# Transformer block on one Trainium2 core: odd channel tiles of the MLP input used as operands where they lie, squares on ScalarE, the first half's residual later, the last stores behind loads

## The chip, the cores and the metric

The kernel runs on one core of a Trainium2 chip. Its time is the device time of one execution, in microseconds (us). The engines are TensorE (PE in the profile, with its weight loads as PEld), VectorE (DVE), ScalarE (ACT), GpSimd (POOL) and SyncE (SP). DMAs are issued from three queues here: SP's (q1 in the profile), ACT's (q10) and POOL's (q0). All move their bytes on the core's 16 DMA engines.

## The reference, cut to what matters

One decoder layer in float32 over 512 positions with 2048 channels. The attention and recurrence in its first part are the same in both kernels. The change is in the MLP and in the residual behind it:

```python
h = rms_norm(x1, norm2_w) * (1 + scale) + shift      # adaLN: scale, shift, gate from c
f = jnp.square(jax.nn.relu(h @ w_ff1))               # 2048 -> 8192
x = x1 + gate * (f @ w_ff2)                          # 8192 -> 2048
```

## The kernel before, in words

Every float32 product is made of three float32r matmuls: an operand is split into `hi` (a cast on ACT) and `lo` (the rest, by a subtraction on DVE), and PE sums hi x hi, hi x lo and lo x hi. A matmul is 128x128 against 128x512.

From about 1000 us on the kernel runs the MLP. FF1 gives 16 groups `g` of 512 hidden columns.

- *Plain groups*, g = 0 to 3, about 1016 to 1190 us (`first_hidden`, then `hidden(g)`). `h2[k]` is the hi/lo pair of channel tile k of the normalised input (128 channels x 512 positions), `uT[k]` the same in float32. A group multiplies the 16 tiles with weights `wraw`, cast to `whi` (ACT) and `wlo` (DVE), into four PSUM banks. Relu goes to an SBUF tile, DVE squares it into `fs`.
- *Forms.* The other 12 groups of FF1 and all of FF2 are done by a Strassen-Winograd scheme with seven products of half-size blocks. Its left operands are seven forms of the four blocks a11, a12, a21, a22 of an activation tile. `make_forms` computes them in `fs`, splits them two at a time into `part` tiles (`plain_stage`, 7 buffers) and stores the parts in DRAM from POOL's queue: `f_hid`, `f_lod` for the hidden groups, `h_hid`, `h_lod` for the input. `input_forms(u)`, u = 0 to 3, does it for four channel tiles of the input each. These tasks are generators; `tick()` takes the next step of one after each channel tile of groups 1 to 3.
- *Form products.* `product(i, ...)` runs product i, in the order 1, 5, 6, 7, 3, 4, 2 (the very first block: 1, 3, 5, 6, 7, 4, 2). It is four turns u of 12 matmuls. `operand` loads the forms from DRAM on POOL's queue as `Fh` and `Fl`, half of them at a time, into four `fp` buffers. For FF1, the forms of products 4 and 2 are loaded once, as `Rh` and `Rl` of 1 MB each (pool `res`), and kept. `part` casts a weight block `raw` (loaded by SP, 512 KB) to `vhi` on ACT and takes `vlo` on DVE. The blocks are b11, b12, b21, b22; b11 and b12 are replaced by sums on DVE in the course of a round, product 2 takes b21 and product 3 takes b22. FF1 has six such blocks of two groups (to about 1680 us). FF2 has two halves `q` of the output columns with four rounds `c` each, a round being seven products.
- *Turn.* After an FF1 block, `turn` transposes the two new groups, squares them (on ACT already) and calls `make_forms` in place: the lo parts are stored from `fs2` itself. The last turn, for group 14, runs in the first round of FF2.
- *Residual.* `residual_in(q)` loads from ACT's queue the gate (one DMA of 128x1024) and eight tiles `d` of x1 (128x512 each), which `finish` in the last round of the half needs. It is issued after the last copy of round c = 0 (`done`).

PE's order is the order of the code. The other engines' order is set by a scheduler that estimates times. A `dma_start` stands in the instruction queue of the engine that issues it: while it waits, all behind it on that engine wait. A DMA also waits for the DMA before it with the same completion semaphore: POOL's DMAs use eight semaphores in turn (DMASW0 to 7), and SP's and ACT's share another eight (DMAHW0 to 7).

Of the kernel before, what the change touches and what calls it, by code (L numbers as in the profile page):

```python
# [15 lines left out]
P = 128  # L16
# [28 lines left out]
def hybrid_block(ctx, tc, x, c, positions, norm1_w, w_ada, b_ada, w_in, q_norm_w, k_norm_w,  # L45
# [92 lines left out]
    def to_cols(accs, dst):  # L138
# [6 lines left out]
        pc = bank("pc")  # L145
# [77 lines left out]
    ph = ctx.enter_context(ExitStack())  # L223
    hp = ph.enter_context(tc.tile_pool(name="hp", bufs=1, side="right"))
# [7 lines left out]
    def pair(i):  # L232

        return [hp.tile([P, S], F32R, name=f"{c}{i}", tag=f"{c}{i}") for c in ("hi", "lo")]
# [5 lines left out]
    for i in range(NK):  # L240
        pair(i)
# [25 lines left out]
    spare.extend(hp.tile([P, 512], F32, name="araw", tag=f"{c}{k}") for k in range(8, NK) for c in ("hi", "lo"))  # L267
# [678 lines left out]
    def first_hidden():  # L946
# [28 lines left out]
        run_all(to_cols(accs, bias))  # L975
# [12 lines left out]
    def hidden(g):  # L988
# [7 lines left out]
        for j in range(4):  # L996
            r = xr.tile([P, 512], F32, name="relu", tag="x")
            act.activation(r, banks[j], AF.Relu)
            yield r
# [10 lines left out]
    def forms_in_dram(name, n):  # L1010
        return [dr.tile([n * FORMS * P, 512], F32, name=f"{name}_{c}d").rearrange("(g i p) n -> g i p n", i=FORMS, p=P)
                for c in ("hi", "lo")]

    fparts, hparts = forms_in_dram("f", NG), forms_in_dram("h", KG)

    def make_forms(fs, dst, g, stage, in_place=False):
# [7 lines left out]
        for a, b in ((0, 2), (2, 4), (4, 6), (6, 7)):  # L1024
            hi = stage()[:, 0:b - a]
            lo = fs[:, a:b].bitcast(F32R) if in_place else stage()[:, 0:b - a]
            act.copy(hi, fs[:, a:b])
            dve.tensor_tensor(lo, fs[:, a:b], hi.bitcast(F32), op=ALU.subtract)
            for d, t in zip(dst, (hi, lo)):
                pool.dma_start(d[g, a:b].rearrange("i p n -> p i n"), t.rearrange("p i a t -> p i (a t)").bitcast(F32))  # L1030
            yield
# [7 lines left out]

    def plain_forms():  # L1040
        return stg.tile([P, FORMS, 2, 256], F32, name="fs", bufs=1)

    def plain_stage():
        return stg.tile([P, 2, 2, 256], F32R, name="part", bufs=7)

    def input_forms(u):
        fs = plain_forms()
        for j in range(4):
            act.copy(block(fs, j), halves(uT[4 * u + j]))
        yield  # L1050
        yield from make_forms(fs, hparts, u, plain_stage)
# [3 lines left out]
    for g in range(PLAIN):  # L1055
# [5 lines left out]
        for j, r in enumerate(rs):  # L1061
            dve.tensor_tensor(block(fs, j), halves(r), halves(r), op=ALU.mult)
# [9 lines left out]
    ph.close()  # L1072
# [10 lines left out]
    res_ = ctx.enter_context(ExitStack())  # L1083
    res = res_.enter_context(tc.tile_pool(name="res", bufs=1, side="right", reuse_waits="tile"))


    slot_of = {1: 1, 2: 3, 3: 6, 4: 2, 5: 4, 6: 5, 7: 0}
    order = (1, 5, 6, 7, 3, 4, 2)
    first_order = (1, 3, 5, 6, 7, 4, 2)
    NC = NG // KG  # L1090
    kept = {}

    def operand(src, c, i):

        def load(t, d, g):
            n = t.shape[1]
            pool.dma_start(t.rearrange("p g a t -> p g (a t)").bitcast(F32),  # L1097
                           d[g:g + n, slot_of[i]].rearrange("g p n -> p g n"))
            return t
# [280 lines left out]
```

## Time and profile before

| | |
|---|---|
| median of 3 runs (lowest, highest) | 2307.28 us (2306.57, 2311.78) |
| profiled execution, its span | 2306.17 us, 2304.4 us |
| mean granted TensorE clock | 0.994 |
| DMA bytes | 606.71 MB, mean 263 GB/s |
| POOL's queue q0 | 262.60 MB |
| SP's queue q1 | 332.54 MB |
| ACT's queue q10 | 9.44 MB |

The span is that of the recorded instructions; 1.8 us of the execution lie around it. A row of the list of waits names the waiting engine, operation and line, then what it waited for: total us, times, longest. In a timeline row stand start, duration, engine, line, operation, out<-in, and in brackets the idle time before it and what ended it. "ACTq" and "SPq" are DMA issues in those queues. A row of DMA issues ends with size and time from issue to landing.

### The profile page before, as it was taken

What the parts mean: (1) busy time and instruction counts of PE and PEld (TensorE: products, weight loads), DVE (VectorE), ACT (ScalarE), POOL (GpSimd) and SP (SyncE); (2) the same over time, 40 slices, a digit from 0 to 9 for tenths busy, and PEclk for the clock granted to TensorE, in tenths of its full rate; (3) what the DMA queues carried; (4) which work ended last, traced back from release to release, by engine and by line L of the source; (5) the groups of instructions that cost most, each with busy time, mean ns of one, the idle gap of its engine ahead of it and who ended that gap; (6) DMA issues with size and microseconds to landing.
All of it is one profiled execution on the core that took longest, in us unless ns stands there. A gap on an engine that the chain in (4) does not pass through costs nothing.

```text
span 2304.4 us, 33163 instructions
## 1 busy us (share of the span) xinstructions
PE 2230.5 (97%) x11769; PEld 1829.2 (79%) x11769; DVE 1825.9 (79%) x2773; ACT 1103.0 (48%) x1958; POOL 458.1 (20%) x668
## 2 busy tenths in 40 slices
PE   4999999999999999999999999999998999999999
PEld 3787877888778888888887888888887888888887
DVE  6899777677776565669767988988895789967878
ACT  5555434433344553457644555565563333344332
POOL 1000022000230000001332323323232222222221
PEclk9999999999999999999999999999999999999999
DMA  9798455556545256746999799889889987999784
GB/s 327 249 337 314 123 176 156 176 162 215 178 149 182 74 186 218 259 132 220 366 382 382 252 341 355 301 297 380 310 295 369 339 288 262 364 336 335 277 302 165
DMA packets 264695, 606.71 MB, mean 263 GB/s; under 512 B 23284, under 2 KB 44032, under 8 KB 264528
## 3 DMA queue, kind: packets, MB, share of 16 engines
q1 hardware_dynamic: 186800, 332.54, 42.8%
q0 software_dynamic: 72832, 262.60, 31.1%
q10 hardware_dynamic: 4896, 9.44, 1.2%
q8 instruction: 93, 1.52, 0.3%
q14 instruction: 74, 0.61, 0.1%
HBM read 522.68 MB, written 81.81 MB: 262 GB/s over the span
## 4 chain that ended last, share of the span: by engine, by line
PE 56%; DMA 16%; DVE 14%; issue 10%; POOL 2%; ACT 1%; SPq 0%; DVEq 0%; POOLq 0%; ACTq 0%
PE f L1160 9%; PE f L1161 9%; PE f L1159 9%; DMA araw<-in_w_ada_dram 7%; PE prj L198 4%; PE prj L200 4%; PE prj L199 4%; DMA f_lod<-fs 3%; DVE acc L129 3%; PE f L208 2%; PE f L206 2%; PE f L207 2%; DVE vlo L1146 2%; DVE wlo L40 2%; PE prj L206 2%
## 5 line engine op out<-in xcount | busy, mean ns | idle before, releaser
L1145 ACT CAST vhi<-raw 128x1024 fp32r<-128x1024 f32 x392 | 412.8, 1055 | 547.1 <-PE f L1161 434.3
L1146 DVE TENSOR_TENSOR vlo<-raw,vhi 128x1024 fp32r<-128x1024 f32 x392 | 477.4, 1225 | 154.3 <-ACT vhi L1145 153.5
L1159 PE MATMUL f<-vhi,Fh 128*128 128x512 f32 x1376 | 537.6, 391 | 8.3 <-DMA Fh<-h_hid 3.6
L1160 PE MATMUL f<-vlo,Fh 128*128 128x512 f32 x1376 | 538.1, 391 | 3.0 <-DVE vlo L1146 3.0
L1161 PE MATMUL f<-vhi,Fl 128*128 128x512 f32 x1376 | 537.2, 390 | 2.1 <-DMA Fl<-f_lod 1.3
L39 ACT CAST whi<-wraw 128x512 fp32r<-128x512 f32 (+1 forms) x368 | 219.8, 601 | 449.3 <-PE prj L200 323.7
L198 PE MATMUL prj<-whi,hi 128*128 128x512 f32 x896 | 365.0, 407 | 1.3 <-ACT gg L698 1.3
L200 PE MATMUL prj<-whi,lo 128*128 128x512 f32 x896 | 351.5, 392 | 0.0
L199 PE MATMUL prj<-wlo,hi 128*128 128x512 f32 x896 | 350.8, 391 | 0.0
L40 DVE TENSOR_TENSOR wlo<-wraw,whi 128x512 fp32r<-128x512 f32 (+1 forms) x368 | 245.1, 670 | 111.7 <-ACT whi L39 107.1
L129 DVE SCALAR_TENSOR_TENSOR acc<-araw,sc,acc 128x512 f32<-128x512 f32 (+1 forms) x392 | 253.9, 678 | 98.5 <-DMA araw<-in_w_ada_dram 97.2
L1159 PEld LDWEIGHTS f<-vhi,Fh 128*128 128x128 f32 x1376 | 259.0, 188 | 63.3 <-issue 7.1
L1160 PEld LDWEIGHTS f<-vlo,Fh 128*128 128x128 f32 x1376 | 259.0, 188 | 61.7 <-DVE vlo L1146 8.3
L1161 PEld LDWEIGHTS f<-vhi,Fl 128*128 128x128 f32 x1376 | 259.1, 188 | 56.7 <-DMA Fl<-f_lod 1.8
L1129 DVE TENSOR_TENSOR raw<-raw,raw 128x1024 f32<-128x1024 f32 x224 | 269.5, 1223 | 1.8 <-DMA raw<-in_w_ff_dram 1.5
L198 PEld LDWEIGHTS prj<-whi,hi 128*128 128x128 f32 x896 | 169.4, 189 | 36.5 <-ACT gg L698 1.6
L200 PEld LDWEIGHTS prj<-whi,lo 128*128 128x128 f32 x896 | 168.9, 188 | 36.8
L199 PEld LDWEIGHTS prj<-wlo,hi 128*128 128x128 f32 x896 | 169.6, 189 | 32.4 <-DVE wlo L40 0.4
L1097 POOL DMA_DIRECT2D Fh<-f_hid x112 | 80.9, 722 | 428.3 <-PE f L1161 414.8
L208 PE MATMUL f<-hi,wlo 128*128 128x512 f32 x256 | 99.8, 390 | 0.6 <-DVE wlo L40 0.6
L206 PE MATMUL f<-hi,whi 128*128 128x512 f32 x256 | 100.2, 391 | 0.0
L207 PE MATMUL f<-lo,whi 128*128 128x512 f32 x256 | 99.6, 389 | 0.0
(306 smaller groups left out, 2956.9 us busy)
## 6 DMA issues: line engine op xcount, KB each, us to landing
raw<-in_w_ff_dram SPq DMA_DIRECT2D x224, 512.0 KB, 10.0
araw<-in_w_ada_dram SPq DMA_DIRECT2D x384, 256.0 KB, 4.3
Fh<-f_hid POOLq DMA_DIRECT2D x112, 512.0 KB, 6.5
Fl<-f_lod POOLq DMA_DIRECT2D x112, 512.0 KB, 7.4
wraw<-in_w_in_dram SPq DMA_DIRECT2D x104, 512.0 KB, 4.1
Fh<-h_hid POOLq DMA_DIRECT2D x60, 512.0 KB, 6.8
Fl<-h_lod POOLq DMA_DIRECT2D x60, 512.0 KB, 8.3
f_hid<-part POOLq DMA_DIRECT2D x48, 512.0 KB, 8.1
```

What stands on the lines that cost most here:

```text
L39: nc.scalar.copy(hi, src)
L40: (eng or nc.vector).tensor_tensor(lo, src, hi.bitcast(F32), op=ALU.subtract)
L129: dve.scalar_tensor_tensor(acc, raw[:, k - k0], vec[:, k:k + 1], acc, op0=ALU.mult, op1=ALU.add)
L198: pe.matmul(banks[ti], lhsT=hi[:, ts], rhs=whi, start=first, stop=False)
L199: pe.matmul(banks[ti], lhsT=hi[:, ts], rhs=wlo, start=False, stop=False)
L200: pe.matmul(banks[ti], lhsT=lo[:, ts], rhs=whi, start=False, stop=last)
L1129: dve.tensor_tensor(dst, a, b, op=ALU.subtract)
L1145: act.copy(hi, src)
L1146: split_done.append(dve.tensor_tensor(lo, src, hi.bitcast(F32), op=ALU.subtract))
L1159: pe.matmul(banks[t], lhsT=fh[u][:, a, ts], rhs=whi[:, a], start=first, stop=False)
L1160: pe.matmul(banks[t], lhsT=fh[u][:, a, ts], rhs=wlo[:, a], start=False, stop=False)
L1161: pe.matmul(banks[t], lhsT=fl[u][:, a, ts], rhs=whi[:, a], start=False, stop=end)
```

## The change

It has four parts.

1. *Odd tiles in place.* In the input's form layout, the odd channel tiles hold a22 and a12, which are the operands of products 4 and 2 as they are. `operand` now hands out slices of `h2`'s odd tiles for these, so the `Rh`/`Rl` loads and the pool `res` go. The pool `hp` of the pairs is split: `hp0` (even tiles) is freed after the plain groups, `hp1` (odd tiles) is kept until the end of the FF1 products. a11 is stored straight from the even tiles; only four forms per u are computed (in `xf`) and split. `part` has 5 buffers instead of 7.
2. *Squares on ACT.* The plain groups' Relu goes from PSUM straight to `fs`, and ACT squares there (`squared`, now shared with `turn`); DVE multiplies group 0's banks by `rbc` in place.
3. *Last stores behind loads.* In FF2 a task step is taken once a product instead of four times, and the stores of group 14 are ordered behind the latest operand load (`behind=loads`).
4. *Residual.* `residual_in(q)` stands at the end of round c = 1 for q = 0 (before: c = 0) and c = 0 for q = 1, and it is ordered behind the last `vhi` cast of product 2 (`cast_done[-1]`) instead of behind the last copy of that product's result.

```diff
-    hp = ph.enter_context(tc.tile_pool(name="hp", bufs=1, side="right"))
+    hp1 = ph1.enter_context(tc.tile_pool(name="hp1", bufs=1, side="right"))
+    hp0 = ph0.enter_context(tc.tile_pool(name="hp0", bufs=1, side="right"))
...
         for j in range(4):
-            r = xr.tile([P, 512], F32, name="relu", tag="x")
-            dve.tensor_tensor(r, banks[j], rbc, op=ALU.mult)
-            act.activation(r, r, AF.Relu, bias=bias[:, j:j + 1])
-            yield r
+            dve.tensor_tensor(banks[j], banks[j], rbc, op=ALU.mult)
+            yield banks[j], bias[:, j:j + 1]
...
+    def split_out(fs, a, b, stage, in_place, dst, behind=None):
+        hi = stage()[:, 0:b - a]
+        lo = fs[:, a:b].bitcast(F32R) if in_place else stage()[:, 0:b - a]
+        act.copy(hi, fs[:, a:b])
+        dve.tensor_tensor(lo, fs[:, a:b], hi.bitcast(F32), op=ALU.subtract)
+        with tc.issue_after(behind[-1].ins) if behind else ExitStack():
+            for d, t in zip(dst, (hi, lo)):
+                pool.dma_start(d.rearrange("i p n -> p i n"), t.rearrange("p i a t -> p i (a t)").bitcast(F32))
...
+    def squared(fs, banks):
+        for j in (0, 2, 1, 3):
+            act.activation(block(fs, j), halves(banks[j][0]), AF.Relu, bias=banks[j][1])
+            if j in (2, 3):
+                v = fs[:, (j - 2) * 2:(j - 2) * 2 + 2]
+                act.activation(v, v, AF.Square)
...
-        return stg.tile([P, 2, 2, 256], F32R, name="part", bufs=7)
+        return stg.tile([P, 2, 2, 256], F32R, name="part", bufs=5)
     def input_forms(u):
-        fs = plain_forms()
-        for j in range(4):
-            act.copy(block(fs, j), halves(uT[4 * u + j]))
-        yield
-        yield from make_forms(fs, hparts, u, plain_stage)
+        xf = stg.tile([P, 4, 2, 256], F32, name="xf", bufs=1)
+        s1, s2, s4, s3 = (xf[:, i] for i in range(4))
+        for a in range(2):
+            ev, od = (halves(uT[4 * u + 2 * a + e]) for e in range(2))
+            a21, a11, a22, a12 = ev[:, 0], ev[:, 1], od[:, 0], od[:, 1]
...
+            for d, t in zip(hparts, h2[4 * u + 2 * a]):
+                pool.dma_start(d[u, 1, :, a * 256:(a + 1) * 256], t[:, 256:512].bitcast(F32))
+        yield
+        for a in (0, 2):
+            split_out(xf, a, a + 2, plain_stage, False, [d[u, 4 + a:6 + a] for d in hparts])
+            yield
...
         if src is hparts and i in (4, 2):
-            if i not in kept:
-                kept[i] = [load(res.tile([P, KG, 2, 256], F32R, name=f"R{n}{i}"), d, 0) for d, n in zip(src, "hl")]
-            return [[t[:, u] for u in range(KG)] for t in kept[i]]
+            half = slice(256, 512) if i == 2 else slice(0, 256)
+            return [[[h2[4 * u + 2 * a + 1][j][:, half] for a in range(2)] for u in range(KG)] for j in range(2)]
...
-                tick()
+                if u == KG - 1 or src is hparts:
+                    tick()
...
-        yield from make_forms(fs, fparts, 2 * b + n, stage, True)
+        yield from make_forms(fs, fparts, 2 * b + n, stage, True, loads if 2 * b + n == NG - 2 else None)
...
                     if c == 0:
-                        done = act.copy(accs7[i, t], banks[t])
+                        act.copy(accs7[i, t], banks[t])
...
-            if c == 0:
-                with tc.issue_after(done.ins):
+            if c == 1 - q:
+                with tc.issue_after(cast_done[-1].ins):
                     residual_in(q)
```

Three places show what moves. First POOL's queue where the form products of FF1 begin, before. Numbers behind a name tell tiles apart; the two pairs at the top belong to the second product, the R tiles to products 4 and 2, the last pair to the third product. `part_12106` and so on hold the forms of group 3.

```order
L1097 DMA Fh_12302<-h_hid_10578 128x2x512
L1097 DMA Fl_12304<-h_lod_10579 128x2x512
L1097 DMA Rh4_12618<-h_hid_10578 128x4x512
L1097 DMA Rl4_12620<-h_lod_10579 128x4x512
L1097 DMA Rh2_12721<-h_hid_10578 128x4x512
L1097 DMA Rl2_12723<-h_lod_10579 128x4x512
L1030 DMA f_hid_10576<-part_12106 128x2x512
L1030 DMA f_hid_10576<-part_12112 128x2x512
L1030 DMA f_lod_10577<-part_12107 128x2x512
L1030 DMA f_hid_10576<-part_12118 128x2x512
L1030 DMA f_lod_10577<-part_12113 128x2x512
L1097 DMA Fh_12372<-h_hid_10578 128x2x512
```

The same place after the change (`Fh_12316` is the third product's first half, `Fh_12320` its second):

```order
L1125 DMA Fh_12246<-h_hid_10581 128x2x512
L1125 DMA Fl_12248<-h_lod_10582 128x2x512
L1023 DMA f_hid_10579<-part_12053 128x2x512
L1125 DMA Fh_12316<-h_hid_10581 128x2x512
L1125 DMA Fl_12318<-h_lod_10582 128x2x512
L1023 DMA f_hid_10579<-part_12059 128x2x512
L1023 DMA f_lod_10580<-part_12054 128x2x512
L1023 DMA f_hid_10579<-part_12065 128x2x512
L1023 DMA f_lod_10580<-part_12060 128x2x512
L1125 DMA Fh_12320<-h_hid_10581 128x2x512
L1125 DMA Fl_12322<-h_lod_10582 128x2x512
```

The R loads are gone, and the third product's first pair stands ahead of all stores of group 3 but one, where it stood behind seven of them.

Next POOL's queue in the first round of FF2 (q = 0, c = 0), where the last turn's parts are stored, before. `Fh_16660` is the first half of product 4's operand and `Fh_16664` its second; `fs2` holds lo parts, `part2` hi parts.

```order
L1030 DMA f_hid_10576<-part2_16446 128x2x512
L1030 DMA f_hid_10576<-part2_16468 128x2x512
L1097 DMA Fh_16660<-f_hid_10576 128x2x512
L1097 DMA Fl_16662<-f_lod_10577 128x2x512
L1030 DMA f_lod_10577<-fs2_16369 128x2x512
L1030 DMA f_hid_10576<-part2_16490 128x2x512
L1030 DMA f_hid_10576<-part2_16524 128x512
L1030 DMA f_lod_10577<-fs2_16369 128x2x512 x2
L1030 DMA f_lod_10577<-fs2_16369 128x512
L1097 DMA Fh_16664<-f_hid_10576 128x2x512
L1097 DMA Fl_16666<-f_lod_10577 128x2x512
```

And after the change (product 4's halves are `Fh_16586` and `Fh_16590`, product 2's `Fh_16671` and `Fh_16675`):

```order
L1125 DMA Fh_16586<-f_hid_10579 128x2x512
L1125 DMA Fl_16588<-f_lod_10580 128x2x512
L1023 DMA f_lod_10580<-fs2_16305 128x2x512 x2
L1125 DMA Fh_16590<-f_hid_10579 128x2x512
L1125 DMA Fl_16592<-f_lod_10580 128x2x512
L1023 DMA f_hid_10579<-part2_16662 128x2x512
L1023 DMA f_lod_10580<-fs2_16305 128x2x512
L1125 DMA Fh_16671<-f_hid_10579 128x2x512
L1125 DMA Fl_16673<-f_lod_10580 128x2x512
L1125 DMA Fh_16675<-f_hid_10579 128x2x512
L1125 DMA Fl_16677<-f_lod_10580 128x2x512
```

Between the halves of product 4's operand stood six stores (a 128x2x512 store is 512 KB, a 128x512 one 256 KB), now two; two more stand ahead of product 2's first half, and the last two behind its second.

Last ACT's order around the residual of q = 0, with the semaphores that each row waits for, before (end of c = 0) and after (c = 1). `raw2_16830` is the fourth block that the next round's first product casts; `raw2_17340` is its first one after the change.

```order
L1320 COPY a21_16174<-f2_16739 128x512 [waits PE_49]
L1272 DMA gate2_16814<-gate2_453 128x1024 [waits DMASW4_49,DMASW5_49,DMASW3_49,DMASW0_49]
L1276 DMA d000_16175<-x1d_9245 128x512
L1276 DMA d001_16176<-x1d_9245 128x512
L1276 DMA d010_16177<-x1d_9245 128x512 [waits DMAHW4_49]
L1276 DMA d011_16178<-x1d_9245 128x512 [waits DMAHW5_49]
L1276 DMA d100_16179<-x1d_9245 128x512 [waits DMAHW6_49]
L1276 DMA d101_16180<-x1d_9245 128x512 [waits DMAHW7_49]
L1276 DMA d110_16181<-x1d_9245 128x512 [waits DMAHW0_49]
L1276 DMA d111_16182<-x1d_9245 128x512 [waits DMAHW1_49]
L1145 CAST vhi_16914<-raw2_16830 128x1024 [waits DVE_49]
```

```order
L1163 CAST vhi_17312<-raw2_16780 128x1024 [waits DMAHW0_49,DVE_49,PE_49]
L1290 DMA gate2_17330<-gate2_456 128x1024 [waits DMASW7_49,DMASW5_49,DMAHW0_49,DMASW4_49,DMASW1_49]
L1294 DMA d000_16111<-x1d_9248 128x512 [waits DMAHW1_49]
L1294 DMA d001_16112<-x1d_9248 128x512 [waits DMAHW2_49]
L1294 DMA d010_16113<-x1d_9248 128x512 [waits DMAHW3_49]
L1294 DMA d011_16114<-x1d_9248 128x512 [waits DMAHW4_49]
L1294 DMA d100_16115<-x1d_9248 128x512 [waits DMAHW6_49]
L1294 DMA d101_16116<-x1d_9248 128x512 [waits DMAHW7_49]
L1294 DMA d110_16117<-x1d_9248 128x512 [waits DMAHW0_49]
L1294 DMA d111_16118<-x1d_9248 128x512 [waits DMAHW1_49]
L1163 CAST vhi_17382<-raw2_17340 128x1024 [waits DVE_49,PE_49]
```

The residual has moved from behind the copy of product 2's result to behind product 2's last cast. The loads of SP that use the same semaphores just before, after the change (`raw2_17340` to `17346` are b11 of the next round, `17364` to `17370` are b21):

```order
L1139 DMA raw2_17340<-in_w_ff2_dram 128x2x512 [waits DMAHW1_49,DVE_49]
L1139 DMA raw2_17342<-in_w_ff2_dram 128x2x512 [waits DMAHW2_49,DVE_49]
L1139 DMA raw2_17344<-in_w_ff2_dram 128x2x512 [waits DMAHW3_49,DVE_49]
L1139 DMA raw2_17346<-in_w_ff2_dram 128x2x512 [waits DMAHW4_49,DVE_49]
L1139 DMA raw2_17364<-in_w_ff2_dram 128x2x512 [waits DMAHW5_49,DVE_49]
L1139 DMA raw2_17366<-in_w_ff2_dram 128x2x512 [waits DMAHW6_49,DVE_49]
L1139 DMA raw2_17368<-in_w_ff2_dram 128x2x512 [waits DMAHW7_49,DVE_49]
L1139 DMA raw2_17370<-in_w_ff2_dram 128x2x512 [waits DMAHW5_49,DVE_49]
```

d100 waits for the semaphore of b21's second load (DMAHW6), d101 for that of the third (DMAHW7). For q = 1 these are b21's first and third.

More of the change, by code (lines that the diff above doesn't have):

```diff
@@ L238, in split_to @@
         dve.tensor_tensor(hl[1], src, hl[0].bitcast(F32), op=ALU.subtract)
-    for i in range(NK):
+    for i in (*range(0, NK, 2), *range(1, NK, 2)):
         pair(i)
@@ L266, in hybrid_block @@
     second_scale = mod_cols(1, 1, g1c, n1c, 256, True)
-    spare.extend(hp.tile([P, 512], F32, name="araw", tag=f"{c}{k}") for k in range(8, NK) for c in ("hi", "lo"))
+    spare.extend((hp0, hp1)[k % 2].tile([P, 512], F32, name="araw", tag=f"{c}{k}")
+                 for k in range(8, NK) for c in ("hi", "lo"))
     for _ in range(8):
@@ L1060, in hybrid_block @@
         fs = plain_forms()
-        for j, r in enumerate(rs):
-            dve.tensor_tensor(block(fs, j), halves(r), halves(r), op=ALU.mult)
+        squared(fs, rs)
         for _ in make_forms(fs, fparts, g, plain_stage):
@@ L1107, in operand @@
             for o, d, n in zip(out_, src, "hl"):
-                t = load(pools["fp"].tile([P, 2, 2, 256], F32R, name=f"F{n}"), d, KG * c + h)
-                o.extend(t[:, u] for u in range(2))
+                t = pools["fp"].tile([P, 2, 2, 256], F32R, name=f"F{n}")
+                g = KG * c + h
+                slot_ = (hslot_of if src is hparts else slot_of)[i]
+                loads.append(pool.dma_start(t.rearrange("p g a t -> p g (a t)").bitcast(F32),
+                                            d[g:g + 2, slot_].rearrange("g p n -> p g n")))
+                o.extend([t[:, u, a] for a in range(2)] for u in range(2))
         return out_
```

64 lines of the change are left out of this document (27 added, 37 removed).

## The prediction

> **What bounds the kernel now.** I read the page's busy times first (two lines), then what TensorE (PE) waited for from 1000 us to the end (total, times, longest), then windows around the few waits.
>
> ```profile
> span 2304.4 us, 33163 instructions
> PE 2230.5 (97%) x11769; PEld 1829.2 (79%) x11769; DVE 1825.9 (79%) x2773; ACT 1103.0 (48%) x1958; POOL 458.1 (20%) x668
> PE f L1159 <- DMA Fh<-h_hid: 3.6, 1, 3.6
> PE f L1160 <- DVE vlo L1146: 3.0, 7, 0.8
> PE f L1159 <- DMA Fh<-f_hid: 2.7, 1, 2.7
> PE f L1159 <- ACT vhi L1145: 2.0, 1, 2.0
> PE f L1161 <- DMA Fl<-f_lod: 1.3, 1, 1.3
> PE f L1161 <- DMA Fl<-h_lod: 0.8, 1, 0.8
> ```
>
> PE is busy 97%, and the change does not touch its matmuls. What can be won are stalls, and from the plain groups on there are three: one for h parts (3.6 and 0.8 us), one for f parts (2.7 and 1.3), one for a vhi cast (2.0, with 0.8 of the vlo row behind it). Work taken off ScalarE (ACT) or VectorE (DVE) gains nothing by itself.
>
> The windows (busy time and count of PE, PEld, DVE, ACT, POOL; then granted clock, DMA share, GB/s):
>
> ```profile
> 1211.00:1222.00 11.00, 6.60 (x22) 4.71 (x21) 11.00 (x11) 2.01 (x2) 3.38 (x5) 0.84 1.03 391
> 1716.00:1740.00 24.00, 24.00 (x108) 19.87 (x107) 15.37 (x15) 13.88 (x17) 11.27 (x16) 1.00 1.02 387
> 1740.00:1750.00 10.00, 5.96 (x19) 4.14 (x18) 1.58 (x2) 1.41 (x2) 1.44 (x2) 0.83 1.04 393
> 1771.00:1776.00 5.00, 2.27 (x9) 1.35 (x8) 2.66 (x3) 3.74 (x4) 0.00 (x0) 1.00 1.04 388
> 1826.00:1842.00 16.00, 16.00 (x72) 13.27 (x71) 10.95 (x11) 6.33 (x6) 4.33 (x6) 1.00 1.04 388
> ```
>
> Read the matmul counts: undisturbed, 108 in 24 us, 0.222 us each. So the first stall (A) costs 11 - 22 x 0.222 = 6.1 us, the second (B) 10 - 19 x 0.222 = 5.8, the third (C) 5 - 9 x 0.222 = 3.0. A and B cost about 1.7 more than their waits; there the granted clock is 0.84 and 0.83. C shows 1.00 and no such extra. The last column but one is the DMA share: the DMA engines are full in all of them.
>
> **The change part by part.** *Odd tiles in place (stall A).* POOL's and PE's instructions in order of time, and the landing time of one R load:
>
> ```profile
> 1183.03 0.77 POOL L1097 DMA_DIRECT2D Rh<-h_hid  x1 [0.71 <-DMA Fh<-h_hid]
> 1190.29 0.75 POOL L1097 DMA_DIRECT2D Rl<-h_lod  x1 [1.96 <-PE f L208]
> 1206.00 0.73 POOL L1097 DMA_DIRECT2D Fh<-h_hid  x1 [1.95 <-DMA Rl<-h_lod]
> Rl<-h_lod POOLq DMA_DIRECT2D x1, 1024.0 KB, 15.2
> 1215.34 0.47 PE L1159 MATMUL f<-vhi,Fh 128*128 128x512 f32 x1 [3.58 <-DMA Fh<-h_hid]
> ```
>
> Four R loads of 1 MB are issued from 1183.03 to 1190.29 (first and last shown); the last takes 15.2 us, and POOL's next F load waits for it and is issued at 1206.00, landing when PE has waited 3.58 us. The change drops these loads. Half of the first block's third F pair then stands ahead of all but one store. Second halves wait for PE to free an F buffer, as everywhere in steady state. Gain 6.1; if another load comes late in its place, 0. I take 6.1, since 4.2 MB leave the queue that was late.
>
> *Last stores behind loads (stall B).* POOL's queue from 1716 to 1746 (packets, MB, share), and the waiting matmul:
>
> ```profile
> q0 software_dynamic: 2058, 7.46, 64.9%
> 1743.44 0.47 PE L1159 MATMUL f<-vhi,Fh 128*128 128x512 f32 x1 [2.71 <-DMA Fh<-f_hid]
> ```
>
> Between the halves of that product's operand stand stores of 2.62 MB before, 1.05 MB after. At q0's 7.46 MB in 30 us, 249 GB/s, 1.57 MB less is 6.3 us earlier, against 2.7 + 1.3 of waiting: the stall goes, 5.8 gained. What is late next is the following product's first half, behind 1.05 MB of moved stores: its Fl lands near 1747.5 by the same rate, about 1 us after its turn. So 0 to 1.1 lost; I take 0.5.
>
> *Residual (stall C, and two new places).* ACT in order of time, and the two raw loads of 1752 to 1776:
>
> ```profile
> 1760.56 1.06 ACT L1145 CAST vhi<-raw 128x1024 fp32r<-128x1024 f32 x1 [1.66 <-PE f L1161]
> 1763.42 0.33 ACTq L1272 DMA_DIRECT2D gate<-gate  x1
> 1763.78 8.44 ACTq L1276 DMA_DIRECT2D d<-x1d  x8
> 1772.26 3.90 ACT L1145 CAST vhi<-raw 128x1024 fp32r<-128x1024 f32 x4 [8.39 <-DMA Fl<-f_lod]
> L1121 SPq DMA_DIRECT2D raw<-in_w_ff_dram x2: 367/368/368, 1752.0 to 1755.2; - x2
> DMA to landing us min/median/max: 15.1/15.7/16.2
> ```
>
> Nine DMAs hold ACT's queue for 8.8 us: the seventh d takes the semaphore of a raw load that lands at 1755.2 + 16.2 = 1771.4, and the vhi cast behind waits. (The name Fl in the cast's row is the profile's guess.) The cast's regular start is 1760.56 + 2.72 = 1763.28; it starts 9.0 us late and PE loses 3.0. So a cast has 6.0 us of cover.
>
> The change gives this place back: 3.0. It puts the nine DMAs behind the last vhi cast of product 2, which runs as that product *starts* on PE: for the first half one column later, for the second half at the same column's end, some 9 us earlier than now. The order shows what waits: the gate and four d's use semaphores of b11's loads, then d100 that of b21's second load (first, for q = 1), d101 that of the third. Behind them on ACT are the next product's casts, and behind these PE.
>
> SP's loads and ACT's casts at the two new places, the old place of the second half, and the three queues from 1764 to 1768:
>
> ```profile
> 1826.03 8.53 SPq L1121 DMA_DIRECT2D raw<-in_w_ff_dram  x4
> raw<-in_w_ff_dram SPq DMA_DIRECT2D x4, 512.0 KB, 10.0
> 1831.84 1.06 ACT L1145 CAST vhi<-raw 128x1024 fp32r<-128x1024 f32 x1 [1.67 <-PE f L1161]
> 1834.56 1.05 ACT L1145 CAST vhi<-raw 128x1024 fp32r<-128x1024 f32 x1 [1.66 <-PE f L1161]
> 2052.26 11.25 SPq L1121 DMA_DIRECT2D raw<-in_w_ff_dram  x5
> raw<-in_w_ff_dram SPq DMA_DIRECT2D x4, 512.0 KB, 10.1
> 2060.81 1.05 ACT L1145 CAST vhi<-raw 128x1024 fp32r<-128x1024 f32 x1
> 2063.04 1.05 ACT L1145 CAST vhi<-raw 128x1024 fp32r<-128x1024 f32 x1 [1.19 <-PE f L1161]
> 2071.58 4.46 ACTq L1276 DMA_DIRECT2D d<-x1d  x8
> q0 software_dynamic: 207, 0.72, 47.4%
> q10 hardware_dynamic: 131, 0.47, 29.7%
> q1 hardware_dynamic: 204, 0.38, 26.6%
> ```
>
> First half: b21's four loads are issued 2.72 us apart from 1826.03, and the third lands at 1831.47 + 10.0 = 1841.5. With d101 and the two d's behind it (1.3 us by the rows of C) the next cast starts at 1842.8; its limit is 1834.56 + 6.0 = 1840.6. Low bound 2.3 us, if the loads land as before. But the DMA engines are full there (share 1.04), and from 1833.0 on the residual adds a third queue. With three queues q1 (the weights) moves 0.38 MB in 4 us, 5.5 us for a load. The two raw loads of C, amid residual DMAs, landed 15.1 and 16.2 us after 1752.0 and 1755.2, 4.3 us apart. Of b21, 3.1 loads are left at 1833.0: at 4.3 us the third lands at 1846.4, the cast starts at 1847.7, and 7.2 us are lost; at 5.5 us, 11.0. I take 4.3, the row of the same event; while PE stands, POOL asks for nothing, which speaks against 5.5.
>
> Second half: d's from 2061.9; the third load, issued near 2060, lands at 2070.0 alone; the limit is 2063.04 + 6.0 = 2069.0. Low bound 2.3; 3.0 loads left at 4.3 us give a cast at 2076.0, 7.0 lost; at 5.5 us, 10.6. Before, this half cost nothing: its d's were issued in 4.46 us, with no load outstanding to wait for. A wait of 7 us I charge with A's and B's 1.7 each for the slow clock.
>
> *Plain groups and input forms.* Per group four Relu straight from PSUM and two Squares (1.05 us each by the vhi casts of the same shape) replace four Relu and four DVE products: some 2 us more ACT per group, DVE relieved; neither ends a wait of PE there in the list above, so 0. Per u, two splits and their four stores go and four half-row stores come, issued by POOL during the first group, when it stores no parts yet: 0. Part buffers fall from 7 to 5; its price is a rival's.
>
> **Sum**, against the profiled execution, 2306.17 us (span 2304.4 and 1.8 around it; the median of the runs is 2307.28, 1.1 above): -6.1 - 5.8 - 3.0 + 0.5 + 7.2 + 7.0 + 3.4 = +3.2, so 2309.4 us. 0.2% is 4.6 us, about what a measurement of this kernel tells from no change: the forecast is no measurable change, three stalls exchanged for two longer ones. With 3.6 to 4.9 us a load it is 2305 to 2313.
>
> **The rivals.** *The residual costs little.* If SP's loads, ahead in their queue, land as before, the two places cost 2.3 each and no clock: -14.9 + 4.6 + 0.5 = -9.8, 2296.4. For it: only the part up to the third load matters. Against it: share 1.04 before a byte is added.
>
> *Three queues take equal turns.* With 5.5 us a load the two places cost 21.6 + 3.4: +10.6, 2316.8, slower. It decides from 4.5 us a load on. For it: in the three-queue rows q0 and q1 took 207 and 204 packets. Against it: POOL's demand ends when PE stops. The Trainium skill, DMA: Bandwidth & Descriptors, Queues, rings and completion order, says that each DMA engine goes round the queues it has work for packet by packet; those two counts agree with that. By that rule taken strictly, with 1.9, 3.5 and 3.6 KB packets from the three rows, q1 gets 21% of 393 GB/s, 6.5 us a load, and the sum would be 2323.
>
> *Five part buffers hold up the casts* (slower).
>
> ```profile
> q0 software_dynamic: 3041, 10.93, 70.9%
> 1105.49 0.63 ACT L39 CAST whi<-wraw 128x512 fp32r<-128x512 f32 x1 [0.20 <-PE f L207]
> ```
>
> (The POOL queue from 1075 to 1115, and a whi cast of the third group.) In the second plain group 3.67 MB of f parts and 8.4 MB of h parts are stored after the change, 12.1 MB. At 10.93 MB in 40 us that is 44 us, as long as the group; the last part cast must wait for the store five back, near 1077 + 9.5 / 0.273 = 1112, and the whi cast near it, which now starts at 1105.5, has until about 1111.5 with the cover of a vhi cast. Price 0.5 to 4 us, and 1.7 of clock: 2312 to 2315. Against it: that cast waited for PE to free its buffer, so the casts run as far ahead as they can.
>
> *Stores or loads are late again in A or B:* 6 us of the gain stays away, 2315.
>
> **How the numbers follow.** Forecast 0.40; residual cheap 0.27; equal turns 0.13; part buffers 0.12; A or B late again 0.08. Faster: the cheap residual and 0.03 of the forecast, 0.30. Same: 0.40, the rest of the forecast and the mild end of the part buffers. Slower: 0.30. The range 2297 to 2317 leaves out about 0.1 at either end.
>
> **What the profile after would show.** Right: no wait of PE for h_hid near 1211 or f_hid near 1743; the nine ACT DMAs just after a vhi cast near 1820 and 2050, d100 and d101 held by raw loads, and PE waiting about 7 us for vhi at each place. Wrong: waits under 3 us there (then faster), a wait of PE for whi in 1060 to 1190, or the old waits still in their places.

## The result: slower by 0.6%, and the profile after

| | before | after |
|---|---|---|
| median of 4 runs (lowest, highest) | 2308.98 us (2306.57, 2311.78) | 2323.85 us (2322.46, 2325.36) |
| profiled execution, its span | 2306.17, 2304.4 us | 2325.36, 2323.6 us |

The ratio is 1.0064 with an interval of 1.0047 to 1.0082: 14.9 us slower between the medians, 19.2 between the two profiled executions (after's lies 1.5 above its median, before's 2.8 below its own). The forecast was 2309.4, the range 2297 to 2317.

The page of the kernel after (span and busy times), and what PE waited for from 1000 us to the end (total, times, longest):

```profile
span 2323.6 us, 33097 instructions
PE 2237.2 (96%) x11769; PEld 1831.6 (79%) x11769; DVE 1811.3 (78%) x2765; ACT 1096.4 (47%) x1942; POOL 447.7 (19%) x664
PE f L1177 <- ACT vhi L1163: 10.6, 2, 6.9
PE f L1178 <- DVE vlo L1164: 8.4, 11, 4.1
PE f L206 <- ACT pc L152: 5.0, 1, 5.0
PE f L208 <- DVE wlo L40: 0.8, 1, 0.8
PE f L1179 <- DMA Fl<-f_lod: 0.2, 1, 0.2
```

The long waits for h_hid and f_hid are gone. Two for vhi stand there, as forecast. Two rows were not forecast: a wait for `pc`, the PSUM tile of `to_cols`, and a vlo wait of 4.1 us. Windows around all these places (columns as in the prediction):

```profile
1060.00:1072.00 12.00, 7.05 (x19) 5.29 (x18) 11.47 (x23) 10.45 (x23) 1.92 (x4) 0.72 0.87 307
1216.00:1228.00 12.00, 12.00 (x54) 9.67 (x53) 12.00 (x12) 3.69 (x4) 4.67 (x7) 1.00 0.96 355
1251.00:1271.00 20.00, 14.89 (x52) 11.35 (x51) 15.07 (x17) 5.04 (x5) 1.41 (x2) 0.83 0.96 346
1748.00:1758.00 10.00, 9.83 (x44) 7.84 (x43) 4.11 (x4) 5.23 (x6) 3.37 (x6) 1.00 1.04 401
1843.00:1854.00 11.00, 6.83 (x19) 4.77 (x18) 6.33 (x7) 3.93 (x5) 1.41 (x2) 0.69 0.97 362
2079.00:2093.00 14.00, 6.66 (x19) 4.66 (x18) 5.95 (x6) 4.85 (x6) 1.41 (x2) 0.63 0.83 310
```

The second and fourth hold A's and B's old places, which lie near 1219 and 1751 in the time of this execution. They run undisturbed, 0.22 us a matmul, but for 0.17 us of waiting at B's. The others hold four stalls: by the count of matmuls 7.8, 8.5, 6.8 and 9.8 us. I call the first two D and E.

A sharper account is possible, because each kernel here has the same 11769 matmuls in nearly the same order: take the start of the n-th matmul in both traces and subtract. The difference is flat to a few tenths of a us between the stalls and steps at each of them. These are the steps, in us, for the kernel after and for the experiments below (columns: places in the time of before; the last is the sum at the end of the profiled execution):

| kernel | to 1050 | D 1066 | A 1211 | E 1255 | B 1743 | next operand | C's place 1772 | residual 1845 | residual 2080 | end |
|---|---|---|---|---|---|---|---|---|---|---|
| after | -0.5 | 8.0 | -5.9 | 8.7 | -6.2 | 0.4 | -3.3 | 7.7 | 10.2 | 19.2 |
| e1 | 5.2 | 7.4 | -5.9 | 8.3 | -6.2 | 0.4 | 13.4 | 0 | 0 | 22.5 |
| e2 | -2.6 | 0 | -5.9 | 7.4 | -6.2 | 0.9 | -3.3 | 6.3 | 11.0 | 7.6 |
| e3 | -5.1 | 7.5 | -5.9 | 3.0 | -6.2 | 0.5 | -3.3 | 11.1 | 7.8 | 9.7 |
| e5 | 1.3 | 0 | -5.9 | 3.0 | -6.2 | 0.9 | -3.3 | 0 | 0 | -10.2 |
| e6 | 1.1 | 0 | -5.9 | 3.0 | -6.2 | 1.3 | -3.3 | 0 | 0 | -9.8 |
| e7 | 0.2 | 0 | -5.9 | 0 | -6.2 | 0.8 | -2.8 | 0 | 0 | -13.9 |
| e8 | 2.6 | 0 | -5.9 | 8.6 | 1.4 | 0 | -1.9 | 0 | 0 | 4.6 |
| e9 | -1.3 | 0 | 0 | 0 | -6.2 | 1.2 | 12.9 | 0 | 0 | 6.6 |
| e10 | 1.1 | 0 | -5.9 | 0 | -6.2 | 0.6 | -3.3 | 0 | 0 | -13.6 |
| e11 | 0.2 | 0 | -5.9 | 0 | 0.9 | 0 | -3.3 | 0 | 0 | -8.1 |

The first column is the MLP's past, which the change does not concern; it lies up to 5 us to either side of before's from execution to execution, and so the medians of many runs carry the verdicts, and the steps say where.

**D.** ACT's first and last row for `pc`, and PE's first matmul behind them and the rows where its pace changes:

```profile
1062.31 0.26 ACT L152 ACTIVATE pc<-pc 128x128 f32<-128x128 f32 x1
1065.72 0.19 ACT L152 ACTIVATION_READ_ACCUMULATOR pc<-pc 128x1 f32 x1
1065.96 0.79 PE L206 MATMUL f<-hi,whi 128*128 128x512 f32 x1 [4.95 <-ACT pc L152]
1071.25 0.63 PE L206 MATMUL f<-hi,whi 128*128 128x512 f32 x1
1071.67 0.52 PE L207 MATMUL f<-lo,whi 128*128 128x512 f32 x1
```

`to_cols` sums the bias columns out of a PSUM bank on ACT, in four steps. In before that bank came from the ring "bg"; the change asks for it from the ring "mm", because group 0's four banks are now held in "bg" until their Relu. But the banks of "mm" are those of the next group: group 1's fourth matmul bank is the one that `pc` holds, and ACT does its four steps between other work, the last at 1065.7. PE stood for 4.95 us, and then went at half its pace until about 1071.7: the last two rows start 0.42 us apart, where 0.22 is regular.

**E.** SP's order at that place, in the first FF1 block (`raw2_12156` to `12162` are this block's b21; `12768`, the last load of b22, and `12754`, the first of b12, are the next block's):

```
L1139 DMA raw2_12768<-in_w_ff1_dram 128x2x512
L1139 DMA raw2_12754<-in_w_ff1_dram 128x2x512
L1139 DMA raw2_12156<-in_w_ff1_dram 128x2x512
L1139 DMA raw2_12158<-in_w_ff1_dram 128x2x512
L1139 DMA raw2_12160<-in_w_ff1_dram 128x2x512
L1139 DMA raw2_12162<-in_w_ff1_dram 128x2x512
```

`12754` needs a buffer that comes free at 1236.4; until then SP stands, and the four b21 loads, which product 4 needs, go out at 1236.8 to 1238.5. In before nothing of the next b12 stood ahead of them and they went out at 1222.7 to 1225.4. DVE's rows behind them, and PE's two waits:

```profile
1247.61 1.22 DVE L1147 TENSOR_TENSOR raw<-raw,raw 128x1024 f32<-128x1024 f32 x1 [0.81 <-DMA raw<-in_w_ff_dram]
1251.97 0.69 DVE L1224 TENSOR_TENSOR s<-s,f 128x512 f32<-128x512 f32 x1 [3.13 <-PE f L1179]
1262.45 3.49 DVE L1164 TENSOR_TENSOR vlo<-raw,vhi 128x1024 fp32r<-128x1024 f32 x3
1253.85 0.50 PE L1178 MATMUL f<-vlo,hi 128*128 128x512 f32 x1 [1.01 <-DVE vlo L1164]
1263.73 0.80 PE L1178 MATMUL f<-vlo,hi 128*128 128x512 f32 x1 [4.10 <-DVE vlo L1164]
```

Two things make vlo late: the sums of raw blocks wait for the loads, and the `s` sum of product 7's result stands ahead of product 4's splits on DVE, where it waits for PE until 1251.97.

**Residual.** ACT's rows at the two new places, and PE's:

```profile
1833.30 0.34 ACTq L1290 DMA_DIRECT2D gate<-gate  x1
1833.68 12.82 ACTq L1294 DMA_DIRECT2D d<-x1d  x8
1846.59 1.99 ACT L1163 CAST vhi<-raw 128x1024 fp32r<-128x1024 f32 x2 [12.39 <-DMA d<-x1d]
1847.69 0.79 PE L1177 MATMUL f<-vhi,Fh 128*128 128x512 f32 x1 [3.70 <-ACT vhi L1163]
2069.85 16.02 ACTq L1294 DMA_DIRECT2D d<-x1d  x8
2085.97 2.94 ACT L1163 CAST vhi<-raw 128x1024 fp32r<-128x1024 f32 x3 [15.09 <-DMA d<-x1d]
2087.07 0.79 PE L1177 MATMUL f<-vhi,Fh 128*128 128x512 f32 x1 [6.88 <-ACT vhi L1163]
```

Nine DMAs hold ACT's queue for 13.2 and 16.5 us, the next cast follows within 0.1 us, and PE waits for it. At the first place d100 and d101 take the semaphores of b21's second and third load, issued at 1830.04 and 1832.76; at the second place those of its first and third, issued at 2063.53 and 2068.97. The third load at each place (size, time to landing):

```profile
raw<-in_w_ff_dram SPq DMA_DIRECT2D x1, 512.0 KB, 12.4
raw<-in_w_ff_dram SPq DMA_DIRECT2D x1, 512.0 KB, 15.6
```

They landed at 1845.2 and 2084.6, and d101 goes out at 1845.19 and 2084.57. The loads that held d100 took 9.0 and 10.2 us, to 1839.0 and 2073.7, and d100 goes out at 1839.05 and 2073.73. At the second place b21's second load landed between the two, at 2079.4.

### The profile page after: what moved, and what is told of

Same layout as the page of the kernel before. It is cut to its first block, busy times and chain, and to the rows that moved or that the text cites. A ratio compares the mean times of both kernels' runs of the same rounds, so it can differ in the third digit from the quotient of the medians.

```text
span 2323.6 us, 33097 instructions
## 1 busy us (share of the span) xinstructions
PE 2237.2 (96%) x11769; PEld 1831.6 (79%) x11769; DVE 1811.3 (78%) x2765; ACT 1096.4 (47%) x1942; POOL 447.7 (19%) x664
## 4 chain that ended last, share of the span: by engine, by line
PE 64%; DVE 15%; DMA 12%; issue 6%; ACT 3%; POOL 1%; SPq 0%; ACTq 0%; DVEq 0%; POOLq 0%
PE f L1178 10%; PE f L1179 10%; PE f L1177 10%; PE prj L198 6%; PE prj L200 6%; PE prj L199 6%; DMA araw<-in_w_ada_dram 6%; DVE vlo L1164 3%; DVE raw L1147 2%; PE f L206 2%; DVE acc L129 2%; PE f L207 2%; PE f L208 2%; DMA Fl<-h_lod 2%; PE prj L207 1%
```

## The experiments

The edits are to the kernel after unless it is said otherwise. All ratios are to the kernel before, on the same chip. The experiments ran on three chips (e1 to e5, e6 to e9, e10 and e11), and so across these groups the ratios are compared, not the medians. Two questions stood: are D and E what they seem, and does the residual cost by its place, its bytes or its semaphores?

**e1: the residual back in its old place.**

```diff
-                        act.copy(accs7[i, t], banks[t])
+                        done = act.copy(accs7[i, t], banks[t])
...
-            if c == 1 - q:
-                with tc.issue_after(cast_done[-1].ins):
+            if c == 0:
+                with tc.issue_after(done.ins):
                     residual_in(q)
```

> The change with its fourth part undone: both residuals at the end of round c = 0 again, behind the last copy of product 2's result. In the profile of the changed kernel the two new places cost PE 5.6 us (near 1844) and 10.1 us (near 2080), clock included. Theory (nine DMAs on ACT run out of semaphores, the casts wait behind them, and PE behind the casts): those two waits go, the wait near 1771 comes back with about 3 us, so 12 to 13 us less than the changed kernel, 2311. Rival (it is the bytes: 2.5 MB per half more on full DMA engines cost PE the same wherever they are issued): within 4 us of the changed kernel, 2320 to 2326, the waits only move to the two ends of c = 0.

Measured 2323.42, ratio 1.0077 (1.0056 to 1.0097): nothing is won. Both new stalls are gone, but the old place, which cost 3 us in before, costs 13.4 more (wait list, then ACT):

```profile
PE f L1177 <- ACT vhi L1163: 13.1, 1, 13.1
1772.50 0.33 ACTq L1290 DMA_DIRECT2D gate<-gate  x1
1772.86 19.55 ACTq L1294 DMA_DIRECT2D d<-x1d  x8
1792.46 3.89 ACT L1163 CAST vhi<-raw 128x1024 fp32r<-128x1024 f32 x4 [19.51 <-DMA d<-x1d]
```

The time is the one that the rival named, but not for a reason that I had written down: here the d's wait for the semaphores of four loads still under way, where in before only two held them up. What the nine DMAs cost is set by how far SP's loads are when they are issued, and that moves with everything else.

**e2: the first group's bias and product as before** (squares still on ACT).

```diff
-        run_all(to_cols(accs, bias, "mm"))
+        run_all(to_cols(accs, bias))
         for j in range(4):
-            dve.tensor_tensor(banks[j], banks[j], rbc, op=ALU.mult)
-            yield banks[j], bias[:, j:j + 1]
+            r = xr.tile([P, 512], F32, name="relu", tag="x")
+            dve.tensor_tensor(r, banks[j], rbc, op=ALU.mult)
+            yield r, bias[:, j:j + 1]
```

> The change with group 0's Relu input as before: DVE multiplies into an SBUF tile, and the bias columns use a bank of the first group's ring instead of one that the second group's products need. Theory (PE's wait of 5.0 us for ACT's bias columns near 1061, 8.0 us with the slow clock, comes from that bank alone): the wait goes, 8 us less, about 2316. Rival (ACT itself is late there, by the Relu and Square that it took over, so PE waits for the next thing from ACT, a whi cast): no more than 2 us less, 2322 or above, with a wait of PE for whi in its place.

Measured 2317.27 (9 runs), ratio 1.0039 (1.0025 to 1.0053), 6.6 us under after. D's window has its 55 matmuls again:

```profile
1060.00:1072.00 12.00, 12.00 (x55) 9.94 (x54) 11.43 (x22) 10.67 (x23) 1.08 (x2) 1.00 0.98 346
```

ACT is as busy there as in the window of after (10.67 us against 10.45), and PE waits no more: D is the bank of `pc`. It was worth 8.0 us in the account, 6.6 between medians and 5.8 by the ratios.

**e3: the first block's b21 loads ahead of the second block's b12.** `weights` gets the last b21 load and orders the second block's b12 behind it.

```diff
-                    nc.sync.dma_start(raw, view[...])
+                    with tc.issue_after(behind.ins) if behind and (e, n) == (0, 1) else ExitStack():
+                        raw_loads.append(nc.sync.dma_start(raw, view[...]))
...
-        w = weights(ff1_s, 0, b * 1024, first_order if first else order)
+        w = weights(ff1_s, 0, b * 1024, first_order if first else order,
+                    raw_loads[15] if b == PLAIN // 2 + 1 else None)
```

> The change, with the second block's b12 loads ordered behind the first block's b21 loads in SP's queue, as they stood in the kernel before. Theory (the 9 us lost near 1252 to 1270, where PE waits for vlo of product 4, come from a b12 load that holds SP's queue 4.5 us for a free buffer ahead of the four b21 loads): most of it goes, 6 to 8.5 us less, about 2316. Rival (DVE's own order does it: the sums of product 7's result stand ahead of product 4's splits and wait for PE): half or more of the 9 us stay, 2319 to 2324.

Measured 2319.18, ratio 1.0058 (1.0036 to 1.0079). By the ratios alone this is not told apart from after's 1.0064; the account shows it. E falls from 8.7 to 3.0, the longest vlo wait from 4.1 to 1.6:

```profile
PE f L1179 <- DVE vlo L1165: 6.7, 11, 1.6
```

DVE's row where the `s` sum stands there:

```profile
1246.85 0.69 DVE L1225 TENSOR_TENSOR s<-s,f 128x512 f32<-128x512 f32 x1 [4.15 <-PE f L1180]
```

So the late loads are two thirds of E, 5.7 us, a little less than the 6 to 8.5 expected. In the rest DVE's order still has the sum wait for PE with splits behind it.

**e5: e2 and e3 together, and the residual spread**, one of its nine DMAs behind the last cast of each product from c = 1 on.

```diff
+        yield
         for (r, n, t), d in sums.items():
...
+            yield
...
+            if c == 1:
+                res = residual_in(q)
...
-            if c == 1 - q:
-                with tc.issue_after(cast_done[-1].ins):
-                    residual_in(q)
+                if 1 <= c < NC - 1:
+                    with tc.issue_after(cast_done[-1].ins):
+                        next(res, None)
```

> The change with group 0 as before, b21's loads first, and each residual spread: one of its nine DMAs behind the last cast of each product from round c = 1 on. Theory (the three gains of 6.1, 5.8 and 3.0 us are real, and the three new losses of 8.0, 9 and 15.7 us are each one of order, not of work): all losses go and the gains stay, 2309 - 14 = 2295, at most 2298. Rival for the residual (each of the nine DMAs waits for a weight load, so casts are late nine times by about a microsecond): 2300 to 2306, with many short waits of PE for vhi.

Measured 2296.15, ratio 0.9951 (0.9932 to 0.9969). No wait for vhi is left in its list.

**e6: the residual in two portions.** As e5, but the gate and four d's stand at the change's own place, and the other four behind the last cast of the next product.

```diff
+            if (r, n, t) == (1, 0, 0):
+                yield
...
+                if (c, j) in ((1 - q, 6), (2 - q, 0)):
+                    with tc.issue_after(cast_done[-1].ins):
+                        next(res, None)
```

> The kernel with all three mended (group 0 as before, b21's loads first), but its residual where the change has it, in two portions: the gate and four d's behind product 2's last cast, the other four d's behind the last cast of the next product. The first portion's five DMAs use the semaphores of the gate's and b11's loads, which have landed by then. Theory (ACT stands only for the semaphores of weight loads still under way, about 5.3 us for each of them): five issues of 0.45 us fit in the 6 us of cover, no wait of PE for vhi above 0.5 us near 1820 and 2050, 2295 to 2298 as with nine single DMAs. Rival (the burst of 1.5 MB on full DMA engines delays what PE needs next): 3 to 5 us at each of the two places, 2302 to 2306.

Measured 2296.45, ratio 0.9937 (0.9918 to 0.9956): as good as e5. Its rows at the first place:

```profile
1822.05 1.06 ACT L1165 CAST vhi<-raw 128x1024 fp32r<-128x1024 f32 x1 [1.66 <-PE f L1181]
1822.21 0.33 ACTq L1293 DMA_DIRECT2D gate<-gate  x1
1822.58 1.91 ACTq L1299 DMA_DIRECT2D d<-x1d  x4
1824.77 1.06 ACT L1165 CAST vhi<-raw 128x1024 fp32r<-128x1024 f32 x1 [1.66 <-PE f L1181]
```

Five DMAs at the same place, with the DMA engines as full (share 1.01 in 1820 to 1845), hold ACT for 2.3 us, and the next cast is on time; nine held it for 13.2. So it is not the place but the semaphores: the fifth d and those behind it are the ones that take those of loads under way. The bytes count in so far as such a load lands later amid them: in after the load that held d101 took 12.4 us, the one issued at 1824.60 took 7.1. At the second place of e6 the last three d's did wait for a load, until 2066.70, and the next cast stood for 5.2 us:

```profile
2068.11 2.96 ACT L1165 CAST vhi<-raw 128x1024 fp32r<-128x1024 f32 x3 [5.17 <-issue]
```

No wait of PE for vhi is in the list all the same: 5.2 us lie within the 6 of cover. So a portion need not be free of waiting; its waiting must be shorter than the cover.

**e7: e5, with all of the second block's loads behind the first block's b21.**

```diff
-                    with tc.issue_after(behind.ins) if behind and (e, n) == (0, 1) else ExitStack():
+                    with tc.issue_after(behind.ins) if behind else ExitStack():
```

> The kernel with all three mended and the residual spread, with all loads of the second block's b12 and b22 (before: b12 alone) ordered behind the first block's b21 loads. Theory (the rest of the loss near 1245 to 1262, about 3 us, is in DVE's order: the scheduler expects b21 late and puts product 7's sums ahead of product 4's; with b21's loads early it does not): 2 to 4 us less, 2292 to 2294. Rival (2 MB of b21 loads then run among the h form loads and PE waits for Fh again near 1200 to 1212): 2296 or more.

Measured 2293.94 (6 runs), ratio 0.9933 (0.9917 to 0.9948). E is gone (0.0 in the account): with the loads ordered so, the scheduler also puts the `s` sums behind one more split, where PE is done with their input and DVE waits for nothing:

```profile
1244.84 1.28 DVE L1226 TENSOR_TENSOR s<-s,f 128x512 f32<-128x512 f32 x2
```

The loads moved as well: the last of b21 lands at 1237.7, where it landed at 1245.7 in e3. So e7 does not part what the loads and what DVE's order did to the last 3 us of E. What is left of PE's waits in the MLP:

```profile
PE f L1180 <- DVE vlo L1166: 2.3, 6, 0.4
PE f L1181 <- DMA Fl<-f_lod: 0.5, 1, 0.5
PE f L208 <- DVE wlo L40: 0.3, 1, 0.3
```

**e8: before with part 1 alone** (odd tiles in place, 5 part buffers; the other three parts as before).

```diff
         if src is hparts and i in (4, 2):
-            if i not in kept:
-                kept[i] = [load(res.tile(...), d, 0) for d, n in zip(src, "hl")]
-            return [[t[:, u] for u in range(KG)] for t in kept[i]]
+            half = slice(256, 512) if i == 2 else slice(0, 256)
+            return [[[h2[4 * u + 2 * a + 1][j][:, half] ...
```

> The kernel before with the first part of the change alone: odd tiles in place, four input forms, five part buffers, split pools. Relu, squares, the last stores and the residual are as before. SP's order has the b12 load ahead of b21's here too. Theory (this part takes away the wait for Fh near 1211, 6.1 us, and brings the wait for vlo near 1252, 7 us, through SP's and DVE's order): no wait for h_hid, a wait for vlo of 4 to 5 us near 1245, and the time of before within 3 us, 2304 to 2309. Rival (the vlo wait comes from the squares on ACT): 6 us less than before, 2300.

Measured 2308.55 (12 runs), ratio 0.9997 (0.9985 to 1.0009). A is gone and E is there:

```profile
PE f L1183 <- DVE vlo L1169: 8.2, 9, 4.1
PE f L1182 <- DMA Fh<-f_hid: 3.2, 1, 3.2
```

So E comes with part 1 by itself, and eats its gain: -5.9 and +8.6 in the account.

**e9: before with part 3 alone** (fewer task steps, last stores behind the loads).

```diff
-                tick()
+                if u == KG - 1 or src is hparts:
+                    tick()
...
-        yield from make_forms(fs, fparts, 2 * b + n, stage, True)
+        yield from make_forms(fs, fparts, 2 * b + n, stage, True, loads if 2 * b + n == NG - 2 else None)
```

> The kernel before with the third part of the change alone: group 14's splits one step a product, its stores behind loads; the residual as before at the end of c = 0. Theory (the wait for Fh of f parts near 1743 goes, 5.8 us, and nothing else moves): 2300 to 2302. Rival (the gate waits for the last of these stores, which now land later, and holds ACT longer at the end of c = 0): the wait for vhi near 1771 grows from 3 us by 3 or more, 2304 to 2312.

Measured 2312.78 (12 runs), ratio 1.0016 (1.0005 to 1.0026). B is gone, and C's place costs 12.9 more:

```profile
PE f L1160 <- ACT vhi L1146: 13.2, 1, 13.2
1757.11 0.33 ACTq L1274 DMA_DIRECT2D gate<-gate  x1
1757.48 19.73 ACTq L1278 DMA_DIRECT2D d<-x1d  x8
1777.24 3.88 ACT L1146 CAST vhi<-raw 128x1024 fp32r<-128x1024 f32 x4 [19.68 <-DMA d<-x1d]
```

The rival had the direction and nearly the time (2304 to 2312), but put it on the gate waiting for the moved stores; the gate goes out at 1757.11, right behind the copies, and it is the d's that wait for loads. Part 3 alone loses; it needs the residual moved or split.

**e10: e7 with Relu and squares as before** (products on DVE).

```diff
-            yield r, bias[:, j:j + 1]
+            act.activation(r, r, AF.Relu, bias=bias[:, j:j + 1])
+            yield r
...
-        squared(fs, rs)
+        for j, r in enumerate(rs):
+            dve.tensor_tensor(block(fs, j), halves(r), halves(r), op=ALU.mult)
```

> The fastest kernel so far (group 0 as before, b21's loads before all of the second block's, residual spread) with the plain groups' Relu and squares as before: Relu into an SBUF tile, squares on DVE. Theory (neither engine ended a wait of PE there, so moving the squares to ACT is worth nothing): within 2 us of 2294, no new wait of PE in 1060 to 1190. Rival (the squares on ACT relieve DVE where group 3's splits meet the first block's): 3 us or more slower, 2297 and up, with waits of PE for vlo near 1195 to 1215.

Measured 2292.87 (5 runs), ratio 0.9936 (0.9923 to 0.9948), where e7 has 0.9933. The squares' engine is worth nothing that these runs can tell, as the prediction had it.

**e11: e7 with part 3 undone.**

```diff
-                if u == KG - 1 or src is hparts:
-                    tick()
+                tick()
...
-        yield from make_forms(fs, fparts, 2 * b + n, stage, True, loads if 2 * b + n == NG - 2 else None)
+        yield from make_forms(fs, fparts, 2 * b + n, stage, True, None)
```

> The same fastest kernel with the third part undone: group 14's splits four times a product, its stores where the scheduler puts them. Theory (the wait for Fh and Fl of f parts near 1733 comes back, 2.7 + 1.3 us and the slow clock, less the 0.5 us that the moved stores cost): 5 to 6 us slower, 2299 to 2300. Rival (with fewer bytes about and the residual later the loads land in time anyway): within 2 us of 2294.

Measured 2297.69, ratio 0.9953 (0.9939 to 0.9966), where e7 has 0.9933: some 4.6 us, a little under the 5 to 6 expected, and with intervals that overlap. Between the spans it is 5.8. B's wait is back:

```profile
PE f L1179 <- DMA Fh<-f_hid: 2.9, 1, 2.9
```

## Why the prediction was wrong, point by point

- *A, B, C and the next operand* held, in mechanism and size: 5.9, 6.2 and 3.3 won and 0.4 lost, where 6.1, 5.8, 3.0 and 0.5 stood in the sum. e8, e11 and e9 show A and B each by its own part.
- *Residual* held in mechanism and total: 7.7 + 10.2 = 17.9 against 7.2 + 7.0 + 3.4 = 17.6. That the total agrees is luck. The waits were smaller than forecast, 3.70 and 6.88 (with 0.47 for a vlo behind each) against 7.2 and 7.0, and the slow clock cost more, 3.5 and 2.9 against 1.7 each. The loads landed 1845.2 - 1839.0 = 6.2 and 2084.6 - 2079.4 = 5.2 us apart, nearer to the rival's 5.5 than to the 4.3 taken. But at the first place the earlier of the two landed sooner than the forecast has it: 1839.0 is 1837.7 in the time of before (after is 1.3 late there by the account), against 1846.4 - 4.3 = 1842.1, and so these two errors offset in part. The cover was longer too: the cast at 1846.59 is 10.7 us behind its regular start (1834.56 and the 1.3), and PE lost 3.7, so 7.0 were covered where 6.0 were taken. Of the three queues' packets in 1836 to 1844 the kernel after shows:

```profile
q0 software_dynamic: 338, 1.25, 41.6%
q10 hardware_dynamic: 396, 1.00, 36.6%
q1 hardware_dynamic: 376, 0.73, 24.6%
```

  Equal in packets within a sixth, unequal in bytes: that agrees with the rule of the Trainium skill, DMA: Bandwidth & Descriptors, Queues, rings and completion order, that an engine goes round its queues packet by packet. At the second place, 2072 to 2084, the counts are 578, 756 and 471 (q0, q10, q1) and not equal; so the agreement is that of one place. What I had set against this rival, that POOL's demand ends when PE stops, hardly came to bear. PE stopped at 1844.0, only 1.2 us before the third load landed, and at 2080.2, with two F loads issued at 2080.27 and 2080.96: POOL's queue still moved 0.82 MB from 2080 to 2084.5.
- *Plain groups and input forms: 0* is the first step that failed, by D's 8.0 us. It asked what the moved Relu and squares cost ACT and DVE, which is indeed nothing (e10). It did not ask about the banks: `to_cols(accs, bias, "mm")` stands in the change, and a tile that moves to another ring makes that ring's next user wait for its last reader. PE wanted the bank back about 2 us after it had written `pc`, at 1061.0, and ACT read it for the last time at 1065.7.
- *A: "if another load comes late in its place, 0"* is the second, by E's 8.7 us. I looked for the late load on POOL alone. It was on SP, where one load of the next block had been ordered ahead of four that were due first, and on DVE (e3, e7). The order of SP and DVE could be read beforehand, like those of POOL and ACT that stand ahead of the prediction.
- *The rivals.* Equal turns came nearer on the loads but is not why the time is longer. That its 2323 with strict turns lies next to the 2323.85 measured is an accident, since neither D nor E is in it. Part buffers: no wait for whi stands in the list. A or B late again: not in their queue; E is a new stall, elsewhere.

Without D and E the sum would have been 19.2 - 8.0 - 8.7 = +2.5 in the profiled executions, where 3.2 was forecast. So D and E, 16.7 us together, are what parts the forecast from these executions (19.2 - 3.2 = 16.0), and the likeliest case held for the places I looked at, with luck in the residual; what was missing were the places to which the order of other queues had changed. e7 takes away D, E and the residual's waits, and is the fastest with e10: 2293.94 us, 0.9933 of before.

## What to carry to other kernels

When a change lets a tile live longer or moves it to another ring of buffers, ask who takes the buffer next and who frees it. When a scheduler sets the order, a change in one queue reorders the others: compare the heads of every queue at each stall that should go, above all for a load that waits for a buffer ahead of loads that are due. DMAs issued from an engine that also computes should be few at a time when their semaphores are shared with long loads: nine in a row held ACT 13 to 20 us, and five 2.3. What such a wait costs PE is only what exceeds the cover of its casts, 6 to 7 us here.

## What the runs showed of the hardware

- A long stall of PE cost more than its wait. In D the matmuls started 0.43 us apart for about 5.7 us after a wait of 4.95 (granted clock 0.50 in 1066.0 to 1071.6), then about 0.22. C's short waits in before, 2.0 and 0.8, cost 3.0 and left the clock at 1.00. D cost 8.0 - 4.95 = 3.0 more than its wait, the second residual place 10.2 - 6.9 = 3.3, with smaller waits in it, where I had charged 1.7. The Trainium skill, TensorE: Matmul & The Clock Gate, What's actually happening, has the array at half its clock after an idle window of about 3.4 us until a busy one has passed, the windows running freely. By that page the slow time would be 3.4 to 6.8 us (an estimate from its window); D's 5.7 agrees. B in before does not fit an idle time of 3.4 us: its waits were 2.71 and 1.32 with two matmuls between them, and the granted clock was 0.57 in 1745.5 to 1748.
- Under three busy queues a 512 KB weight load landed 5.2 to 6.2 us behind the one before it, and each DMA on ACT's queue that took the semaphore of a load still under way went out within 0.1 us of that load's landing (in after, e1 and e9).
